# Two blocks of an attention and mixture-of-experts network on one core: block 1's recurrence taken two chunks at a time, and heads' products issued in pairs

## The chip, the cores and the metric

The kernel runs on one core of a Trainium2 chip. The metric is the device time of one launch in microseconds (us); the comparison is between medians of several launches. TensorE is called PE, VectorE DVE, ScalarE ACT, GpSimd POOL and SyncE SP, as the profile calls them.

## The reference, cut to what matters

The input is one sequence of 512 tokens of width 1024. Block 1 projects it (`h @ w_in`), runs a gated recurrence (HGRN2) and a differential attention beside each other, gates and mixes both, and then runs a mixture of experts. Block 2 does the same with an RWKV-7 recurrence and a sparse attention (DSA), followed by a cross attention and a second mixture of experts. The change touches three of these parts:

```
def hgrn2_chunked(q, k, v, log_f):          # 4 heads of 128, 8 chunks of 64 tokens
    def step(state, inp):
        scores = where(causal, q_rel @ k_rel^T, 0)          # 64 x 64 per head
        o = scores @ v + (q * exp(b)) @ state
        new_state = exp(b_end) * state + k_end^T @ v         # 128 x 128 per head
        return new_state, o
o_hg = rms_norm(o, hg_out_norm) * silu(og)

def block(i):                                # differential attention, 4 heads, 128 queries
    a = softmax(q1 @ k1^T) - lam * softmax(q2 @ k2^T)       # q, k of 64 features
    return a @ v
o_da = rms_norm(o_da, da_out_norm) * (1 - lam_init)

s = q_lat @ c_sel^T                          # DSA, 8 heads of 64 features, masked softmax
a = sigmoid(a0 + xa @ a2); w = w0 + tanh(xw) @ w2            # RWKV-7: two products of 64 inner
```

## The kernel before, in words

Everything is float32. A large projection is computed by `mm3` (L209 in the profile): three 128x512 matmuls for each 128 rows of weights, on a high and a low part of each operand. A text that says **dense matmul** means one of these. The weights arrive from HBM in slots and are split by ACT (L194) and DVE (L195). All other matmuls have plain float32 operands, and the trace shows each of them as two passes. Four PSUM banks, d0 to d3, belong to the projections of block 1; the other four, a0 to a3, to the small work.

The order of the instructions on every engine is not written out: a scheduler (the Tile framework with a simulated timeline) places them when the kernel is built. It takes an instruction as soon as its inputs and its buffers are ready in its own simulation, so that PE fills the waits of the small work with dense matmuls. `keep_in_program_order` ties an instruction to the one issued before it in the program. `bank("a")` takes the next bank of a rotation, which `banks(...)` sets.

Block 1 (`dense1`) projects q and k, v, the recurrence's inputs, four gates (`gate(i)`, L691) and the output gate `og`, 1056 dense matmuls in all. `ev_og` takes the four banks of `og` through a Tanh (L700), multiplies on DVE (L701) and then on POOL by the recurrence's normed output (L702), and only with that are d0 to d3 free for `ev_da` and `ev_hg`, the two output projections of 96 dense matmuls each.

The attention (L546 to L571) goes over four heads and four blocks of 128 queries. For each it multiplies the two halves of 64 features (m = 0 and 1), into bank a0 for the one and a1 for the other (L550), adds the mask (L551), runs the softmax, transposes the result through bank a2 (L564) and multiplies by v (L568). Sums of squares for the norm follow for all heads at the end (`tok_sums`, L308).

The recurrence has bank a3 for itself. It goes over four steps of 128 tokens (m), each with scores (L643) and transposes (L648) for two chunks of 64, and then takes the chunks p = 0 and 1 one after the other: state products with 64 inner rows (L658), the state update on DVE (L661), and for every head a product of scores and v (L666) and one of state and q (L667). Its norm (`out_norm`, L677 to L683) follows at the end with its own sums and their spread over the features (`tok_spread`, L319).

Block 2 (`dense2`) runs two small products of 64 inner rows in the RWKV part (L1322, L1326). DSA goes over four pairs of heads (p) and four blocks of queries: scores of the two heads in three banks by turns (L1679), mask (L1682), softmax (L1684 to L1689), transposes through another bank (L1692) and the product with v into d3 (L1698).

## Time and profile before

| | us |
|---|---|
| three launches | 2192.49, 2194.12, 2199.74 |
| median | 2194.12 |
| the profiled execution, device time | 2193.93 |
| its span in the trace | 2192.2 |
| PE busy | 2116.7 (97% of the span) |
| mean granted PE clock | 0.981 of full speed |
| block 1 from its dense matmul #384 to #1056 | 110.9 to 369.2 |
| block 1's output projections | 369.2 to 416.6 |

The profiled execution lies 0.2 us under the median, and 1.7 us of it lie outside the span. The profile gives for each engine its busy time, for each group of instructions its mean time, and for any stretch the granted clock of PE.

### The profile page before, as it was taken

What the parts mean: (1) busy time and instruction counts of PE and PEld (TensorE: products, weight loads), DVE (VectorE), ACT (ScalarE), POOL (GpSimd) and SP (SyncE); (2) the same over time, 40 slices, a digit from 0 to 9 for tenths busy, and PEclk for the clock granted to TensorE, in tenths of its full rate; (3) what the DMA queues carried; (4) which work ended last, traced back from release to release, by engine and by line L of the source; (5) the groups of instructions that cost most, each with busy time, mean ns of one, the idle gap of its engine ahead of it and who ended that gap; (6) DMA issues with size and microseconds to landing.
All of it is one profiled execution on the core that took longest, in us unless ns stands there. A gap on an engine that the chain in (4) does not pass through costs nothing. (4 is left out here: it accounts for less than half of the span.)

```text
span 2192.2 us, 29816 instructions
## 1 busy us (share of the span) xinstructions
PE 2116.7 (97%) x11946; PEld 1363.0 (62%) x11946; DVE 983.7 (45%) x2002; ACT 679.4 (31%) x1317; POOL 161.6 (7%) x138
## 2 busy tenths in 40 slices
PE   8999999999999999998989999999898999999996
PEld 6766778787544444445766775677778454444443
DVE  4674323563333332325388484445455232333334
ACT  5463333253111111114534333433443111111112
POOL 0420001200000000000252100001110000000000
PEclk9999899999999999998999999999999999999998
DMA  4211131377999999993222112112633899999994
GB/s 178 87 66 48 46 109 67 143 287 269 415 419 417 420 420 419 420 377 106 68 76 77 40 63 77 39 65 77 250 110 141 345 409 420 420 419 420 419 419 162
DMA packets 96318, 505.87 MB, mean 231 GB/s; under 512 B 21088, under 2 KB 26208, under 8 KB 44464
## 3 DMA queue, kind: packets, MB, share of 16 engines
q1 hardware_dynamic: 90992, 490.09, 56.3%
q10 hardware_dynamic: 4688, 11.66, 1.5%
q0 software_dynamic: 496, 2.17, 0.3%
q8 instruction: 96, 1.57, 0.3%
q14 instruction: 46, 0.38, 0.0%
HBM read 494.83 MB, written 8.91 MB: 230 GB/s over the span
## 5 line engine op out<-in xcount | busy, mean ns | idle before, releaser
L209 PE MATMUL ps_d<-wslot,xg 128*64 128x512 f32 x2048 | 446.4, 592 | 0.0
L209 PE MATMUL ps_d<-hT,wh 128*128 128x512 f32 x1056 | 348.0, 414 | 1.9 <-DVE hT L300 1.9
L209 PEld LDWEIGHTS ps_d<-wslot,xg 128*64 128x64 f32 x2048 | 148.3, 137 | 286.5 <-issue 276.5
L195 DVE TENSOR_TENSOR wl<-wslot,wh 128x512 fp32r<-128x512 f32 x236 | 168.6, 719 | 287.4 <-ACT wh L194 232.0
L194 ACT ACTIVATE wh<-wslot 128x512 fp32r<-128x512 f32 x260 | 163.2, 630 | 320.9 <-PE ps_d L209 255.8
L209 PEld LDWEIGHTS ps_d<-hT,wh 128*128 128x128 f32 x1056 | 199.7, 195 | 54.7 <-issue 9.3
L1010 DVE TENSOR_TENSOR s<-ps_d,s 128x512 f32<-128x512 f32 x32 | 22.1, 692 | 423.0 <-PE ps_d L209 423.0
L209 PE MATMUL ps_d<-hT,wl 128*128 128x512 f32 x528 | 210.3, 410 | 0.5 <-DVE wl L195 0.5
L209 PE MATMUL ps_a<-wslot,hidT 128*64 128x512 f32 (+1 forms) x832 | 178.3, 578 | 1.7 <-ACT hidT L1018 1.4
L209 PE MATMUL ps_d<-wh,hT 128*128 128x512 f32 x512 | 164.1, 397 | 3.0 <-DVE hT L300 1.4
L1048 DVE TENSOR_TENSOR acc<-acc,ps_a 128x512 f32<-128x512 f32 (+1 forms) x214 | 131.2, 664 | 54.9 <-PE ps_a L209 54.7
L209 PEld LDWEIGHTS ps_a<-wslot,hidT 128*64 128x64 f32 x832 | 58.7, 137 | 108.9 <-issue 100.4
L209 PE MATMUL ps_a<-yy,S 128*128 128x512 f32 (+1 forms) x428 | 114.6, 400 | 5.6 <-DVE acc L1048 5.6
L209 PEld LDWEIGHTS ps_d<-hT,wl 128*128 128x128 f32 x528 | 102.7, 195 | 25.4 <-issue 1.9
L209 PEld LDWEIGHTS ps_d<-wh,hT 128*128 128x128 f32 x512 | 95.7, 188 | 26.7 <-ACT wh L194 1.7
L985 ACT ACTIVATE xg<-ps_a,gain 128x256 f32<-128x256 f32 x102 | 48.2, 475 | 200.0 <-PE ps_a L209 200.0
L209 PE MATMUL ps_a<-oh,xs 128*128 128x256 f32 x816 | 107.1, 285 | 1.3 <-DVE oh L1137 1.3
L209 PEld LDWEIGHTS ps_a<-oh,xs 128*128 128x128 f32 x816 | 100.9, 191 | 9.6 <-issue 9.6
L1036 ACT ACTIVATE yy<-ps_a,gc 128x512 fp32r<-128x512 f32 (+1 forms) x52 | 34.9, 671 | 223.7 <-PE ps_a L209 192.2
L209 PE MATMUL ps_d<-wl,hT 128*128 128x512 f32 x256 | 101.8, 397 | 1.8 <-DVE wl L195 1.8
L209 PEld LDWEIGHTS ps_a<-yy,S 128*128 128x128 f32 x428 | 74.8, 188 | 31.4 <-DVE acc L1048 13.6
L1009 ACT ACTIVATE s<-ps_d 128x512 f32<-128x512 f32 x32 | 19.1, 598 | 199.3 <-PE ps_d L209 199.3
(584 smaller groups left out, 2838.2 us busy)
## 6 DMA issues: line engine op xcount, KB each, us to landing
wslot<-in_wm_dram SPq DMA_DIRECT2D x380, 1024.0 KB, 11.6
wslot<-in_wd_dram SPq DMA_DIRECT2D x108, 512.0 KB, 3.6
wslot<-in_wd_dram SPq DMA_DIRECT2D x19, 1024.0 KB, 14.7
wslot<-in_wm_dram SPq DMA_DIRECT2D x8, 512.0 KB, 15.0
C<-in_x_dram SPq DMA_DIRECT2D x4, 512.0 KB, 5.2
acc<-in_x_dram ACTq DMA_DIRECT2D x4, 512.0 KB, 4.8
kvd<-kvs ACTq DMA_DIRECT2D x8, 256.0 KB, 4.1
xd<-acc ACTq DMA_DIRECT2D x1, 2048.0 KB, 11.9
```

Of the source, the lines that this page charges most:

```text
L194: self.nc.scalar.activation(hi, src, AF.Copy)
L195: (lo_eng or self.nc.vector).tensor_sub(lo, src, hi.bitcast(F32))
L209: self.pin(self.nc.tensor.matmul(*a, **k))
L985: nc.scalar.activation(xg[:, k, :n], b[:, :n], AF.Copy, scale=gain[:, k:k + 1])
L1009: nc.scalar.activation(s1, hb[0], AF.Silu)
L1010: nc.vector.tensor_mul(s1, hb[1], s1)
L1036: nc.scalar.activation(y[0][:, c], b, AF.Copy, scale=gcol)
L1048: nc.vector.tensor_add(acc[:, t, c], acc[:, t, c], b)
```

## The change

A new helper issues a list of products in reversed order and ties all but the first to program order. It is meant for two products with 64 inner rows each, which use the lower and the upper half of PE's rows. Since only the second of two is tied, the scheduler may still put other work between them.

```
+    def side_by_side(self, xs, stop=True):
+        for j, (o, l, r) in enumerate(xs[::-1]):
+            i = self.nc.tensor.matmul(o, l, r, start=True, stop=stop)
+            if j:
+                self.tc.keep_in_program_order(i)
```

In the attention the two score products go through it, into two banks of a rotation of a0 to a3; the transposes reuse the first of these banks, and each head's squares and sums follow its product with v.

```
-                for m in range(2):
-                    r = slice(m * 64, (m + 1) * 64)
-                    b = self.bank("a%d" % m)
-                    nc.tensor.matmul(b[:, :n], qkT[r, 0, h, qs], qkT[r, 1, h, :n], start=True, stop=False)
+                ps, sb = [], [self.bank("a") for _ in range(2)]
+                self.side_by_side([(sb[m][:, :n], qkT[m * 64:m * 64 + 64, 0, h, qs], qkT[m * 64:m * 64 + 64, 1, h, :n])
+                                   for m in range(2)], stop=False)
...
-                b = self.bank("a2")
+                b = sb[0]
...
+            sq = k4([128, 512])
+            nc.scalar.activation(sq, b, AF.Square)
+            b = self.bank("a", (128, 4, 2))
+            self.tok_sums(b, sq, 0, one2)
+            nc.vector.tensor_copy(rd[:, :, 2 * h:2 * h + 2], b)
```

The recurrence loses its own bank and uses the same rotation. A step takes 128 tokens: the state products of both chunks in pairs, eight state updates, one output bank with a product over 128 inner rows of the masked scores (whose off-diagonal halves were zeroed once by POOL) and the products of both states, one copy and one square of the whole step, and its sums.

```
-        self.banks("a3")
...
+            Ss = [S]
+            bks = [self.bank("a", (128, 4, 128)) for _ in range(2 if m < 3 else 1)]
+            for h in range(4):
+                hc = slice(h * 128, (h + 1) * 128)
+                self.side_by_side([(bk[:, h, :], ke[rs[p], h, :], hv[rs[p], m, hc]) for p, bk in enumerate(bks)])
+            for p, bk in enumerate(bks):
+                S = B.tile([128, 4, 128], F32, name="hgS", bufs=3)
+                for h in range(4):
+                    nc.vector.scalar_tensor_tensor(S[:, h, :], Ss[p][:, h, :], eend[:, h, 2 * m + p:2 * m + p + 1],
+                                                   bk[:, h, :], op0=ALU.mult, op1=ALU.add)
+                Ss.append(S)
+            bo = self.bank("a", (128, 4, 128))
+            for h in range(4):
+                nc.tensor.matmul(bo[:, h, :], hv[:, m, h * 128:(h + 1) * 128], sc[:, h, :], start=(h == 0), stop=False,
+                                 skip_group_check=True)
             for p in range(2):
...
                 for h in range(4):
...
+                    nc.tensor.matmul(bo[:, h, rs[p]], Ss[p][:, h, :], qe[:, h, cs[p]], start=False, stop=(p == 1 and h == 3),
+                                     skip_group_check=True)
+            nc.scalar.activation(oT[:, :, tok], bo, AF.Copy)
+            sq = k2([128, 4, 128])
+            nc.scalar.activation(sq, bo, AF.Square)
```

In block 2 the two products of the RWKV part and DSA's scores go through the helper; DSA's pairs alternate between d0, d1 and d2, a2, the transposes reuse the bank of the scores, and the product with v alternates between d3 and a3.

```
-                    b = self.bank(("d0", "d1", "a2")[(turn + e) % 3])
-                    nc.tensor.matmul(b[:, :n], qT[r, p, qs], KT[r, p, :n], start=True, stop=False)
-                    sb.append(b)
+                sb = [self.bank((("d0", "d1"), ("d2", "a2"))[turn % 2][e]) for e in range(2)]
+                turn += 1
+                self.side_by_side([(sb[e][:, :n], qT[e * 64:e * 64 + 64, p, qs], KT[e * 64:e * 64 + 64, p, :n])
+                                   for e in range(2)], stop=False)
...
-                    b = self.bank(("d2", "a3")[turn % 2])
```

**The order on PE, in the recurrence.** The next rows are PE's order of before around one chunk of the recurrence (bank a3); `ps_d...` with hT and wh or wl are dense matmuls of a gate.

```order
L209 MATMUL ps_d2_2321<-hT0_91,wh_2409 128x512
L209 MATMUL ps_d2_2321<-hT1_92,wh_2409 128x512
L209 MATMUL ps_d2_2321<-hT0_91,wl_2410 128x512
L666 MATMUL ps_a3_1898<-k2_1879,F_1534 128x64
L667 MATMUL ps_a3_1898<-E_1389,hgS_1855 128x64
L666 MATMUL ps_a3_1898<-k2_1879,F_1534 128x64
L667 MATMUL ps_a3_1898<-E_1389,hgS_1855 128x64
L666 MATMUL ps_a3_1898<-k2_1879,F_1534 128x64
L667 MATMUL ps_a3_1898<-E_1389,hgS_1855 128x64
L666 MATMUL ps_a3_1898<-k2_1879,F_1534 128x64
L667 MATMUL ps_a3_1898<-E_1389,hgS_1855 128x64
L209 MATMUL ps_d3_2322<-hT0_91,wh_2409 128x512
```

The next rows are PE's order of the change in the recurrence's first and second step (L684 is state and q, L656 the scores, L663 the transposes, L691 the sums, L680 scores and v, L215 the pairs). The dense matmuls at their head are the last of the output gate.

```order
L209 MATMUL ps_d3_2591<-hT0_91,wh_2712 128x512
L209 MATMUL ps_d3_2591<-hT1_92,wh_2712 128x512
L209 MATMUL ps_d3_2591<-hT0_91,wl_2713 128x512
L684 MATMUL ps_a0_1788<-E_1380,hgS_1778 128x64 x4
L656 MATMUL ps_a2_1810<-acc_61 64x64 x8
L663 MATMUL ps_a3_1821<-cst_62,D_1235 128x128 x4
L691 MATMUL ps_a1_1804<-one2_680,k2_1802 128x2 x4
L680 MATMUL ps_a2_1848<-k3_1747,F_1525 128x128 x4
L684 MATMUL ps_a2_1848<-E_1380,hgS_1783 128x64 x4
L215 MATMUL ps_a1_1829<-F_1525,k2_1826 128x128
L215 MATMUL ps_a0_1828<-F_1525,k2_1826 128x128
```

Before, the eight products of a chunk stood between dense matmuls. Now the whole recurrence from here on stands in one row, with no dense matmul among it: dense #1056 is the last one ahead of it.

**The order at the recurrence's end, on PE and ACT.** The next rows are PE's order of the change where the last step ends and the projection of the attention (`ps_d0` from C) begins.

```order
L691 MATMUL ps_a1_1924<-one2_680,k2_1922 128x2 x4
L215 MATMUL ps_a0_1948<-F_1525,k2_1946 128x128 x4
L680 MATMUL ps_a1_1958<-k3_1747,F_1525 128x128 x4
L684 MATMUL ps_a1_1958<-E_1380,hgS_1903 128x64 x4
L684 MATMUL ps_a1_1958<-E_1380,hgS_1953 128x64 x4
L691 MATMUL ps_a2_1974<-one2_680,k2_1972 128x2 x4
L209 MATMUL ps_d0_2754<-C_1196,wh_2760 128x512 x2
L209 MATMUL ps_d0_2754<-C_1196,wl_2761 128x512
```

On ACT the change has this row there (L686 the step's copy, L688 its square, L713 the Tanh of the output gate, L549 the norm's square root, L194 splits).

```order
L686 ACTIVATE G_1742<-ps_a1_1958 128x4x128
L688 ACTIVATE k2_1972<-ps_a1_1958 128x512
L713 ACT_TABLE_LOAD
L713 ACTIVATE k2_2728<-ps_d0_2588 128x512
L713 ACTIVATE k2_2734<-ps_d1_2589 128x512
L713 ACTIVATE k2_2740<-ps_d2_2590 128x512
L549 ACT_TABLE_LOAD
L549 ACTIVATE onr_1745<-onr_1745,eps_65 128x32
L194 ACTIVATE D_2586<-k2_2728 128x512
L194 ACTIVATE D_2586<-k2_2734 128x512
L713 ACT_TABLE_LOAD
L713 ACTIVATE k2_2746<-ps_d3_2591 128x512
```

Before, ACT had this row at the output gate (L700 its Tanh, L679 the norm's square root).

```order
L679 ACT_TABLE_LOAD
L679 ACTIVATE onr_1976<-ps_a3_1977,eps_65 128x32
L194 ACTIVATE wh_2734<-wslot_2716 128x512
L194 ACTIVATE wh_2782<-wslot_2780 128x512
L194 ACTIVATE wh_2798<-wslot_2780 128x512
L700 ACT_TABLE_LOAD
L700 ACTIVATE k2_2750<-ps_d0_2610 128x512
L700 ACTIVATE k2_2756<-ps_d1_2611 128x512
L700 ACTIVATE k2_2762<-ps_d2_2612 128x512
L194 ACTIVATE wh_2816<-wslot_2814 128x512
L194 ACTIVATE D_2608<-k2_2750 128x512
L700 ACTIVATE k2_2768<-ps_d3_2613 128x512
```

The Tanh of the output gate, which frees d0 to d3, now stands behind the last square of the recurrence, and the norm's square root between its third and its fourth Tanh.

**The order on PE, at DSA's end.** The next rows are PE's order of the change in DSA's last two blocks of queries (L215 a pair of scores, L1691 the mask, L1700 transposes, L1705 the product with v; the first row is the last dense matmul of the projection beside it).

```order
L209 MATMUL ps_a1_11178<-r_10011,wl_11198 128x512
L1700 MATMUL ps_a2_10672<-cst_62,k3_10690 128x128 x2
L1700 MATMUL ps_d0_10701<-cst_62,k3_10709 128x128 x3
L1705 MATMUL ps_a3_10644<-GG1_10253,X2_8907 64x128 x4
L215 MATMUL ps_a2_10736<-VU_10008,qT_8933 128x512
L215 MATMUL ps_d2_10735<-VU_10008,qT_8933 128x512
L1691 LDWEIGHTS X4_7459
L1691 MATMUL ps_d2_10735<-X4_7459 128x512
L1691 LDWEIGHTS X4_7459
L1691 MATMUL ps_a2_10736<-X4_7459 128x512
L1705 MATMUL ps_a3_10644<-GG1_10253,X2_8907 64x128
L1700 MATMUL ps_d1_10702<-cst_62,k3_10721 128x128 x3
```

Before, PE's order at the product with v of the last head pair was this one.

```order
L1698 MATMUL ps_d3_10690<-GG1_10275,X2_8929 64x128 x5
L1692 MATMUL ps_a3_10813<-cst_62,k3_10809 128x128 x4
L1698 MATMUL ps_d3_10690<-GG1_10275,X2_8929 64x128
L209 MATMUL ps_a0_11193<-r_10033,wh_11197 128x512
L209 MATMUL ps_a0_11193<-k_10034,wh_11197 128x512
L209 MATMUL ps_a0_11193<-r_10033,wl_11198 128x512
L209 MATMUL ps_a0_11193<-r_10033,wh_11197 128x512
L209 MATMUL ps_a0_11193<-k_10034,wh_11197 128x512
```

The last dense matmul of the projection beside DSA now stands ahead of DSA's last pair, and behind it 16 transposes, 18 products with v, the pair and two masks follow before the next projection begins. Before, 48 dense matmuls stood behind the last transposes, 27 of them behind the last product with v. In the whole order of the change 15 of DSA's 16 pairs stand next to each other, 5 of the attention's 16 (one of 128 and four of 256 keys), all 12 of the recurrence, and one of the four in the RWKV part.

## Rows read from the trace of the kernel before

**Rows 1.** The page, busy time and share of PE.

```profile
PE 2116.7 (97%) x11946; PEld 1363.0 (62%) x11946; DVE 983.7 (45%) x2002; ACT 679.4 (31%) x1317; POOL 161.6 (7%) x138
```

**Rows 2.** Stretches: us, busy us (count) of PE, PEld, DVE, ACT, POOL, granted clock, DMA.

```profile
110.90:369.20 258.30, 257.82 (x1193) 191.30 (x1192) 109.49 (x234) 107.38 (x219) 11.22 (x8) 0.95 0.19 64
369.20:416.60 47.40, 46.87 (x205) 36.86 (x203) 31.52 (x45) 15.81 (x27) 12.22 (x8) 1.00 0.26 87
1343.70:1450.00 106.30, 106.30 (x518) 66.96 (x518) 46.41 (x149) 47.87 (x125) 0.00 (x0) 1.00 0.14 45
```

**Rows 3.** Groups by line in 110 to 420 us: busy us, mean ns.

```profile
L667 PE MATMUL ps_a<-E,hgS 128*128 128x64 f32 x64 | 14.3, 307 | 0.0
L666 PE MATMUL ps_a<-k,F 64*128 64x64 f32 x64 | 13.8, 296 | 0.0
...
L658 PE MATMUL ps_a<-F,k 64*128 64x128 f32 x56 | 8.3, 286 | 0.0
L308 PE MATMUL ps_a<-one,k 128*128 128x2 f32 x64 | 8.3, 256 | 0.0
...
L661 DVE SCALAR_TENSOR_TENSOR hgS<-hgS,eend,ps_a 128x128 f32<-128x128 f32 x28 | 7.9, 342 | 6.9 <-PE ps_a L658 6.8
...
L702 POOL TENSOR_TENSOR k<-k,G 128x512 f32<-128x512 f32 x4 | 5.8, 1455 | 216.2 <-PE ps_a L319 209.4 <-DVE G L683 6.8
L643 PE MATMUL ps_a<-acc 128*64 128x64 f32 x64 | 3.5, 231 | 0.0
...
L700 ACT ACTIVATE k<-ps_d 128x512 f32<-128x512 f32 x4 | 2.2, 599 | 2.2 <-DVE E L195 2.2
...
L700 ACT ACT_TABLE_LOAD x1 | 1.3, 1283 | 0.0
```

**Rows 4.** Timeline of PE, one chunk of the recurrence: start, us, engine, line.

```profile
249.09 0.62 PE L209 MATMUL ps_d<-hT,wh 128*128 128x512 f32 x2
249.65 0.43 PE L666 MATMUL ps_a<-k,F 64*128 64x64 f32 x2
...
252.19 1.68 PE L308 MATMUL ps_a<-one,k 128*128 128x2 f32 x8
```

**Rows 5.** Busy time and granted clock of two neighbouring stretches there.

```profile
249.10:252.40 3.30, 3.30 (x19) 2.47 (x17) 0.69 (x1) 1.88 (x2) 0.00 (x0) 1.00 0.29 94
252.50:259.20 6.70, 6.70 (x21) 5.64 (x21) 0.52 (x2) 1.30 (x3) 0.00 (x0) 0.50 0.08 28
```

**Rows 6.** Timeline of PE at the lower clock, dense matmuls in steps.

```profile
202.42 1.05 PE L209 MATMUL ps_d<-hT,wh 128*128 128x512 f32 x2
203.27 0.84 PE L564 MATMUL ps_a<-cst,k 128*128 128x128 f32 x3
```

**Rows 7.** Timeline of PE, sums of squares at the full clock.

```profile
239.34 1.40 PE L308 MATMUL ps_a<-one,k 128*128 128x2 f32 x12
240.67 1.16 PE L658 MATMUL ps_a<-F,k 64*128 64x128 f32 x8
```

**Rows 8.** Timeline of PE, two products on different halves of its rows.

```profile
206.82 0.37 PE L658 MATMUL ps_a<-F,k 64*128 64x128 f32 x1
206.82 0.48 PE L550 MATMUL ps_a<-C 64*128 64x256 f32 x1
...
207.45 0.23 PE L551 MATMUL ps_a<-dgn,idb 128*128 128x128 bf16 x1
```

**Rows 9.** Timeline of all engines, score products and a reduction in DSA.

```profile
1434.38 0.91 PE L1679 MATMUL ps_a<-VU,qT 64*128 64x384 f32 x2
1435.21 0.44 PE L1692 MATMUL ps_d<-cst,k 128*128 128x128 f32 x2
...
1435.74 1.12 PE L1679 MATMUL ps_d<-VU,qT 64*128 64x512 f32 x2
1436.80 0.39 PE L1682 MATMUL ps_d<-X 128*128 128x512 bf16 x1
...
1437.23 0.69 DVE L1684 TENSOR_REDUCE st<-ps_d 128x1 f32<-128x512 f32 x1 [0.29 <-PE ps_d L1682]
```

More of the change, by code (lines that the diff above doesn't have):

```diff
@@ L569, in dense1 @@
             nc.scalar.activation(vh, b.rearrange("p (j n) -> p j n", j=4), AF.Copy)
[L570 removed]
+            sq = k4([128, 512])
[3 more added lines that the diff above has]
+            nc.vector.tensor_copy(rd[:, :, 2 * h:2 * h + 2], b)
         yd = big("C", (128, 2, 4, 512), F32R)
         vv = lambda h: dv[:, :, h * 128:(h + 1) * 128]
[L573 to L574 removed]
+        scales(rd)
         for h in range(4):
[L576 to L582 removed]
+            b = self.tok_spread(rd, 2 * h, 1)
             o = k3([128, 512])
@@ L634, in dense1 @@
         oT = big("G")
-        S = B.tile([128, 4, 128], F32, name="hgS", bufs=2)
+        S = B.tile([128, 4, 128], F32, name="hgS", bufs=3)
         nc.vector.memset(S, 0.0)
+        rh = A.tile([128, 4, 8], F32, name="onr", bufs=2)
+        scs = [k3([128, 4, 128]) for _ in range(2)]
+        for t in scs:
+            nc.gpsimd.memset(t, 0.0)
         for m in range(4):
             tok = slice(m * 128, (m + 1) * 128)
+            cs = [slice(m * 128 + p * 64, m * 128 + p * 64 + 64) for p in range(2)]
+            rs = [slice(p * 64, p * 64 + 64) for p in range(2)]
             b = self.bank("a", (128, 4, 64))
@@ L641, in dense1 @@
                 for p in range(2):
-                    c = slice(m * 128 + p * 64, m * 128 + p * 64 + 64)
-                    nc.tensor.matmul(b[p * 64:(p + 1) * 64, h, :], krel[:, h, c], qrel[:, h, c], start=True, stop=True)
-            sc = k2([128, 4, 64])
-            nc.vector.tensor_mul(sc, b, self.c("inc64")[:, None, :].broadcast_to([128, 4, 64]))
+                    nc.tensor.matmul(b[rs[p], h, :], krel[:, h, cs[p]], qrel[:, h, cs[p]], start=True, stop=True)
+            sc = scs[m % 2]
+            for p in range(2):
+                nc.vector.tensor_mul(sc[rs[p], :, rs[p]], b[rs[p]],
+                                     self.c("inc64")[rs[p], None, :].broadcast_to([64, 4, 64]))
             b = self.bank("a", (128, 4, 128))
@@ L669, in dense1 @@
-        self.d("o_hgT", oT)
-        def out_norm(o, gcol, out):
-            r = A.tile([128, 4, 8], F32, name="onr", bufs=2)
-            b = self.bank("a", (128, 4, 8))
-            for h in range(4):
-                sq = k2([128, 512])
-                nc.scalar.activation(sq, o(h), AF.Square)
-                self.tok_sums(b, sq, 2 * h, one2)
-            nc.scalar.activation(r, b, AF.Sqrt, scale=1.0 / 128, bias=self.eps)
-            nc.vector.reciprocal(r, r)
-            for h in range(4):
-                b = self.tok_spread(r, 2 * h, 1)
-                nc.vector.scalar_tensor_tensor(out(h), o(h), gcol, b, op0=ALU.mult, op1=ALU.mult)
@@ new lines, in dense1 @@
+            nc.scalar.activation(oT[:, :, tok], bo, AF.Copy)
+            sq = k2([128, 4, 128])
+            nc.scalar.activation(sq, bo, AF.Square)
+            b = self.bank("a", (128, 8))
+            for h in range(4):
+                nc.tensor.matmul(b[:, 2 * h:2 * h + 2], sq[:, h, :], one2, start=True, stop=True)
+            nc.vector.tensor_copy(rh[:, m, :], b)
+        self.d("o_hgT", oT)
+        scales(rh)
+        for h in range(4):
+            b = self.tok_spread(rh, 2 * h, 1)
+            nc.vector.scalar_tensor_tensor(oT[:, h, :], oT[:, h, :], gh[:, 0:1], b, op0=ALU.mult, op1=ALU.mult)
@@ L1320, in dense2 @@
             pc = slice(p * 128, (p + 1) * 128)
-            b = self.bank("a")
-            nc.tensor.matmul(b, lora[0:64, pc], xw[0:64], start=True, stop=True)
+            wb = [self.bank("a") for _ in range(2)]
+            self.side_by_side([(wb[e], lora[e * 64:e * 64 + 64, pc], xw[e * 64:e * 64 + 64]) for e in range(2)])
             ld = tmp[:, p, 0]
-            nc.scalar.activation(ld, b, AF.Tanh, scale=0.5, bias=hw0[:, p:p + 1])
-            b = self.bank("a")
-            nc.tensor.matmul(b, lora[64:128, pc], xw[64:128], start=True, stop=True)
+            nc.scalar.activation(ld, wb[0], AF.Tanh, scale=0.5, bias=hw0[:, p:p + 1])
             th = tmp[:, p, 1]
-            nc.scalar.activation(th, b, AF.Tanh, scale=0.5, bias=ha0[:, p:p + 1])
+            nc.scalar.activation(th, wb[1], AF.Tanh, scale=0.5, bias=ha0[:, p:p + 1])
             nc.gpsimd.tensor_scalar(ld, ld, hc, hc, op0=ALU.mult, op1=ALU.add)
@@ L1670, in dense2 @@
         for p in range(4):
-            bo_ = self.bank("d3")
+            bo_ = self.bank(("d3", "a3")[p % 2])
             for i in range(4):
@@ L1693, in dense2 @@
                     nc.scalar.activation(pTs[:, e, i, :n], b[:, :n], AF.Copy)
-                    turn += 1
                 for j in range(i + 1):
```

39 lines of the change are left out of this document (7 added, 32 removed).

## The prediction, written before the changed kernel ran

> **What bounds the kernel now.** I read the page first: PE is busy for 2116.7 of 2192.2 us, 97% [rows 1], and DVE follows with 45%. So time is won where PE does less or does it at a higher clock, and lost where it has to wait. Then the stretches that the change touches [rows 2]. In block 1, from 110.9 to 369.2 us, PE is busy for 257.82 of 258.30 us, but its granted clock is 0.95; in the output projections behind it and in DSA PE is as full, at 1.00, so that there too PE time saved is time saved. The reader is to see that the small work's waits on DVE and ACT cost nothing there: dense matmuls stand in every gap. Last I read how the clock falls. [...] In block 1 I count eight such stretches of 3.4 us (27.2 us at 0.50 make a mean of 0.947, the 0.95 of the row), each behind a burst of L666, L667 or L308, short matmuls that stand together. A dense matmul there takes 427 ns (202.42 to 203.27 us for two, [rows 6]), at the full clock some 230 (the output projections: 205 matmuls, nearly all of them dense, in 46.87 us, [rows 2]).
>
> **What block 1 loses.** L666 and L667 take 2.54 us a chunk when they stand in a burst [rows 4], eight times 20.3 us; their busy times, which overlap, sum to 28.1 us [rows 3]. I take 23, nearer to the burst, since most chunks are one. L658 goes (8.0, little under its busy 8.3), L643 (3.2 of 3.5) and L648 (16 passes, 1.8, as L308 takes 0.11 us a pass at full clock: 1.33 us for 12, [rows 7]), and the recurrence's half of L308, 32 passes, 3.6. Together 39.6 us. With the bursts gone I also take the eight half-clock stretches away: 3.4 us hold eight dense matmuls of 427 instead of 231 ns, 1.56 us each, 12.5 in all. Of the attention's pairs only five stand next to each other in the new order. A single score product takes 0.83 us for 384 keys (1434.38 to 1435.21) and 1.06 for 512 [rows 9], so 0.22 for 128 keys: about 0.61 for 256 and 0.39 for 128. That two products on different halves of the rows run beside each other is seen once: L658 and L550 both begin at 206.82 us, and all four passes are over at about 207.45 [rows 8], when one L550 of 256 keys alone would take 0.61 us. So a pair costs one product: five pairs give 0.39 + 4 x 0.61 = 2.8 us. Block 1 loses 54.9 us.
>
> **What block 1 gains.** The order shows that from the last dense matmul of the output gate, #1056, to the end of the recurrence no dense matmul is left to fill in. The reason stands in ACT's row: the Tanh that empties banks d0 to d3 comes behind the recurrence's last square. So this stretch is the sum of PE's work and its waits. By the passes (L308's 0.111 us; L643 0.05, 3.2 us for 64), a step of 128 tokens has 8 passes each of scores and v, state one, state two, transposes and sums, 0.9 each or 4.4 with the transposes a little cheaper; 16 passes of scores, 0.8; four pairs, 1.1 (L658's 8.3 us are 0.15 a pass, eight passes one after the other). 6.3 us in all. Behind the pairs PE waits for the first state's four updates: 0.35 us until DVE starts (0.43 after the start of the last matmul that it waits for, [rows 9]), four times 342 ns [rows 3] and, an estimate by the first, 0.1 back to PE, 1.8 us. A step then is 8.1 us at full clock and, with PE's part at 1.92 times, 13.9 at half clock. Which? The stretch is one long burst of the kind behind which the clock fell, so I let it fall in the middle of the second step: 11.0 there, 13.9 in the third, and 12.1 in the fourth, where the wait lies behind two other groups. With the first step's products at the full clock (2.9), the last state's (1.7) and the tail (ACT's copy, square and Tanh at 0.6 each like L700, a table load of 1.28 [rows 3], DVE's product of 0.69 like its reduction in [rows 9], hand-overs 0.65: 4.4) this makes 46.0 us. Ahead of #1056 stand the first scores and transposes, 1.6. The dense matmuls behind begin at half clock, 2.0 (eight to ten of them). Then bank d3 comes late: its Tanh needs a buffer that POOL frees. From the spread's first bank, DVE's product of 0.7, POOL's 1.45 [rows 3], a split of 1.3 (a pass of ACT and one of DVE), the table load and Tanh of 1.9 and DVE's 0.7, with 1.75 of first matmuls and hand-overs, are 7.8 us, of which PE fills 4.5 with the rest of the spread and five dense matmuls; 3.3 remain. Block 1 gains 52.9 us, and so is 2.0 faster in sum.
>
> [...] The shortest passes decide this sum: L308 streams two columns and takes 0.111 us a pass [rows 7]. [...]
>
> **Block 2.** In DSA 15 of 16 pairs stand together. One group of four lengths costs 0.39 + 0.61 + 0.83 + 1.06 = 2.9 us, four times 11.5; without the one pair of 256 keys, 10.9 us less. In the RWKV part one pair of four gives 1.05, the price of one product of 512 columns. A product with 64 inner rows between dense matmuls also costs something at its entry: two dense matmuls ahead of L666 take 0.56 instead of 0.46 us (249.09 to 249.65, [rows 4]). Twenty-one entries fewer, 2.0 us. Against this, DSA's last part has no filler any more: 48 dense matmuls stood behind its last transposes and none do now. Its chain from the last dense matmul on is five transposes and four products with v (2.0 us), the pair and masks (1.6), a softmax of 512 keys and the rest of the other head's (the reduction is 0.69 [rows 9], the exponential about the same, then it is read, inverted and scaled: 3.3 with hand-overs, an estimate by these passes), transposes and copy 1.5, eight products 1.7, and copy and split of the next operand 2.6: 12.7 us. PE has 9.0 of work in it, 3.7 are wait, and with some of the work at half clock I take 4.5 (0 if the next projection's operands come early, 8 if all of it runs at half clock). Sum: -10.9 - 1.05 - 2.0 + 4.5 = -9.5 us.
>
> **The sum.** -2.0 - 9.5 = -11.5 us against the profiled 2193.93, which is 0.2 under the median: about 2182. Both MoE parts and the transfers keep their order, so the shift carries through to the end.
>
> **The rivals.** (a) The clock stays at 1.00 in the recurrence's stretch: 8.1 + 8.1 + 6.6 + 2.9 + 0.9 + 4.4 = 31.0 us instead of 46.0, and 2.0 less behind it, 17 us: **2165**. For it speaks that the stretch has no idle long enough to be seen; against it, that the clock fell behind bursts a tenth as long. (b) The clock is low from the first step (+3) and the attention, with its own L308 and short matmuls, keeps four of the eight half-clock stretches (+6): **2191**, within what can be told. (c) In the stretch nothing overlaps: beside the 1.8 us, the mask (0.9), the transposes' copy (1.0), the output's copy and square (1.6) and the second state's updates wait one after the other, and a step at half clock takes 12.1 + 1.8 + 0.9 + 1.0 + 1.6 + 1.8 = 19 us instead of 14. That is 57 + 9 = 66 us, 20 more: **2202**, slower. It decides from 17.8 us a step on (2200.5). The order speaks against it: sums and the next scores stand between. (d) The pairs don't run beside each other: 10.9 + 1.05 + 2.8 + 2.0 and 4.8 in the recurrence come back, 21.5: **2203**. Against it stands the one overlap at 206.82, for it that this is only one.
>
> **How the numbers follow.** A difference under 0.3%, 6.6 us, can't be told from no change here. My own case has 0.50 and its own range is 2176 to 2189 (the stretch between 42 and 49 us, DSA's tail between 0 and 8); 0.44 of it lies under 2187.5. (a) has 0.15, (b) 0.17, (c) 0.11, (d) 0.07. The range from 2163 to 2196 leaves (c) and (d) out. Faster: 0.44 + 0.15 = 0.59; same 0.06 + 0.17 = 0.23; slower 0.18.
>
> **What the changed profile would show.** Block 1 from dense #384 to #1248 takes about as long as before (305 us). Between #1056 and #1057 there are some 45 us without L209, with a clock of about 0.55; 31 us at 1.00 would be (a), 60 and more (c). Before it, the clock up to #1056 is 1.00; with 0.50 stretches still there, (b). A DSA pair of 512 keys takes 1.06 us, not 2.1 (d). Behind DSA's last dense matmul PE is idle for about 4 us. I would be wrong most of all in the clock of the recurrence, which alone is worth 17 us, and in the half-clock stretches that I let go, 12.5 us.

## The result, and the profile after

The changed kernel takes 2170.49 us (median of 4 launches, 2167.89 to 2170.81) against 2195.49 us before (4 launches): ratio 0.9885, 95% interval 0.9868 to 0.9902, 25 us or 1.15% faster. The forecast was 2182, 11.5 us faster, with a range from 2163 to 2196; the time lies in it, three fifths of the way from the forecast to its low end, and the gain is a little over twice the one forecast. The profiled execution took 2170.49 us, its span is 2168.5 us.

The page of the changed kernel answers to [rows 1]: PE is 37 us less busy and its share of the span is a little lower.

```profile
PE 2079.4 (96%) x11910; PEld 1348.1 (62%) x11914; DVE 986.8 (46%) x2014; ACT 676.4 (31%) x1313; POOL 162.5 (7%) x140
```

To see where the time went I take the starts of the same dense matmuls (L209, 128x512) in both traces, counted from the kernel's first one. The forecast column is the prediction's sum by place: the 54.9 us that block 1 loses and 0.5 for the attention's entries, less 1.6 ahead of #1056; the 46.0 us of the recurrence's stretch; 2.0 and 3.3 behind it; and block 2's terms.

| stretch of PE (starts of dense matmuls) | before, us | after, us | difference | forecast |
|---|---|---|---|---|
| start to #384 | 110.5 | 109.2 | -1.3 | 0 |
| #384 to #1056: attention, and before the recurrence too | 258.3 | 204.8 | -53.5 | -53.8 |
| #1056 to #1057: the bare recurrence | 0.8 | 25.6 | +24.8 | +46.0 |
| #1057 to #1248: output projections | 46.6 | 56.0 | +9.4 | +5.3 |
| #1248 to #4022: first MoE, block 2's RWKV part | 910.0 | 917.4 | +7.4 | -1.2 |
| #4022 to #4313: DSA | 141.2 | 129.2 | -12.0 | -8 |
| #4313 to the end | 724.7 | 726.3 | +1.6 | 0 |

The windows of the changed kernel answer to [rows 2] and [rows 5]. Columns: stretch, length, busy us and count of PE, PEld, DVE, ACT and POOL, granted clock of PE, DMA share and GB/s.

```profile
109.30:314.40 205.10, 205.10 (x952) 153.49 (x951) 104.52 (x216) 95.37 (x201) 13.14 (x10) 1.00 0.22 75
314.40:339.70 25.30, 20.97 (x214) 18.98 (x212) 9.94 (x32) 9.30 (x16) 0.00 (x0) 0.96 0.23 84
339.70:344.50 4.80, 4.80 (x11) 3.76 (x12) 1.53 (x4) 1.77 (x3) 0.00 (x0) 0.50 0.00 0
344.50:354.50 10.00, 5.74 (x33) 4.62 (x31) 5.97 (x8) 3.66 (x5) 4.19 (x3) 0.99 0.00 1
354.50:360.00 5.50, 5.41 (x17) 4.29 (x18) 3.23 (x6) 2.42 (x4) 1.67 (x1) 0.69 0.28 93
```

The attention's stretch runs at 1.00 throughout: the eight half-clock stretches are gone. The recurrence is bare, as the order told, but its clock is 0.96, not 0.55: in this profile it falls only at the stretch's end, at 337.9 us (e1, below, has it earlier). What is lost behind it is the low clock (339.7 to 344.5) and a wait of 4.3 us. One step of the recurrence, in the rows of PE and DVE:

```profile
318.34 1.00 PE L684 MATMUL ps_a<-E,hgS 128*128 128x64 f32 x8
319.27 1.16 PE L215 MATMUL ps_a<-F,k 64*128 64x128 f32 x16
320.48 2.15 DVE L675 SCALAR_TENSOR_TENSOR hgS<-hgS,eend,ps_a 128x128 f32<-128x128 f32 x8 [2.77 <-PE ps_a L215]
320.88 1.21 PE L684 MATMUL ps_a<-E,hgS 128*128 128x64 f32 x8 [0.45 <-DVE hgS L675]
```

PE waits 0.45 us and not 1.8: the first head's product starts at 320.88 us, 0.05 us behind the end of the first of the four updates (320.83) and ahead of the fourth's (321.35). And the wait for bank d3:

```profile
348.73 4.19 POOL L715 TENSOR_TENSOR k<-k,G 128x512 f32<-128x512 f32 x3 [44.91 <-DVE G L697]
...
350.05 0.63 ACT L194 ACTIVATE D<-k 128x512 fp32r<-128x512 f32 x1 [8.55 <-POOL k L715]
...
351.28 0.63 ACT L194 ACTIVATE D<-k 128x512 fp32r<-128x512 f32 x1 [0.60 <-POOL k L715]
351.93 1.28 ACT L713 ACT_TABLE_LOAD   x1
353.22 0.60 ACT L713 ACTIVATE k<-ps_d 128x512 f32<-128x512 f32 x1
...
354.59 0.94 PE L209 MATMUL ps_d<-C,wh 128*128 128x512 f32 x2 [4.35 <-DVE k L714]
```

The chain is the one forecast; the second split (351.28), which stands ahead of the table load on ACT and waits for POOL, was left out of it.

In DSA a pair of 512 keys and the end stand in PE's timeline, which answers to [rows 9].

```profile
1433.39 0.69 PE L215 MATMUL ps_a<-VU,qT 64*128 64x512 f32 x1
1433.40 0.69 PE L215 MATMUL ps_d<-VU,qT 64*128 64x512 f32 x1
1433.92 0.59 PE L215 MATMUL ps_a<-VU,qT 64*128 64x512 f32 x1
1433.93 0.59 PE L215 MATMUL ps_d<-VU,qT 64*128 64x512 f32 x1
1434.68 0.38 PE L1691 MATMUL ps_a<-X 128*128 128x512 bf16 x1 [0.16 <-issue]
...
1442.24 0.96 PE L209 MATMUL ps_d<-GG,wh 128*128 128x512 f32 x3 [1.20 <-ACT GG L194]
```

Both products of the pair start 0.01 us apart and are over after 1.1 us, the time of one (1.12 us in [rows 9]); in the records of the 15 pairs the starts are 6 to 8 ns apart. From here to the next projection PE waits for ACT and DVE four times (0.58, 0.62, 0.24 and 1.20 us), and once ahead of the pair (0.41), 3.05 us in all.

### The profile page after: what moved, and what is told of

Same layout as the page of the kernel before. It is cut to its first block, busy times and chain, and to the rows that moved or that the text cites. A ratio compares the mean times of both kernels' runs of the same rounds, so it can differ in the third digit from the quotient of the medians.

```text
span 2168.5 us, 29754 instructions
## 1 busy us (share of the span) xinstructions
PE 2079.4 (96%) x11910; PEld 1348.1 (62%) x11914; DVE 986.8 (46%) x2014; ACT 676.4 (31%) x1313; POOL 162.5 (7%) x140
## 5 line engine op out<-in xcount | busy, mean ns | idle before, releaser
L209 PE MATMUL ps_d<-wslot,xg 128*64 128x512 f32 x2048 | 446.4, 592 | 0.0
L209 PE MATMUL ps_d<-hT,wh 128*128 128x512 f32 x1056 | 344.2, 410 | 2.8 <-DVE hT L308 2.8
L209 PEld LDWEIGHTS ps_d<-wslot,xg 128*64 128x64 f32 x2048 | 148.3, 137 | 286.5 <-issue 277.1
L194 ACT ACTIVATE wh<-wslot 128x512 fp32r<-128x512 f32 x260 | 163.2, 631 | 310.0 <-PE ps_d L209 239.8
L209 PEld LDWEIGHTS ps_d<-hT,wh 128*128 128x128 f32 x1056 | 197.5, 193 | 54.4 <-issue 9.3
L209 PE MATMUL ps_d<-hT,wl 128*128 128x512 f32 x528 | 205.7, 402 | 0.0
L209 PE MATMUL ps_a<-wslot,hidT 128*64 128x512 f32 (+1 forms) x832 | 178.3, 578 | 1.7 <-ACT hidT L1031 1.4
L209 PE MATMUL ps_d<-wh,hT 128*128 128x512 f32 x512 | 163.8, 397 | 3.1 <-ACT wh L194 1.4
L1061 DVE TENSOR_TENSOR acc<-acc,ps_a 128x512 f32<-128x512 f32 (+1 forms) x214 | 131.2, 664 | 54.9 <-PE ps_a L209 54.7
L209 PEld LDWEIGHTS ps_a<-wslot,hidT 128*64 128x64 f32 x832 | 58.7, 137 | 108.9 <-issue 100.4
L209 PE MATMUL ps_a<-yy,S 128*128 128x512 f32 (+1 forms) x428 | 114.6, 400 | 5.6 <-DVE acc L1061 5.6
L209 PEld LDWEIGHTS ps_d<-hT,wl 128*128 128x128 f32 x528 | 101.3, 192 | 24.0 <-issue 1.5
L209 PEld LDWEIGHTS ps_d<-wh,hT 128*128 128x128 f32 x512 | 95.6, 188 | 26.9 <-ACT wh L194 1.8
L209 PE MATMUL ps_a<-oh,xs 128*128 128x256 f32 x816 | 107.1, 285 | 1.4 <-DVE oh L1150 1.4
L209 PEld LDWEIGHTS ps_a<-oh,xs 128*128 128x128 f32 x816 | 100.9, 191 | 9.6 <-issue 9.6
L209 PE MATMUL ps_d<-wl,hT 128*128 128x512 f32 x256 | 101.3, 396 | 1.8 <-DVE wl L195 1.8
L209 PEld LDWEIGHTS ps_a<-yy,S 128*128 128x128 f32 x428 | 74.8, 188 | 31.4 <-DVE acc L1061 13.5
## 6 DMA issues: line engine op xcount, KB each, us to landing
wslot<-in_wd_dram SPq DMA_DIRECT2D x19, 1024.0 KB, 15.2
```

What stands on the lines that cost most here:

```text
L194: self.nc.scalar.activation(hi, src, AF.Copy)
L209: self.pin(self.nc.tensor.matmul(*a, **k))
L1061: nc.vector.tensor_add(acc[:, t, c], acc[:, t, c], b)
```

## The experiments

Each ran against the kernel before, on one chip for both. The stages are those of the table above; block 1 and bare are lengths, in us.

| run | median, us | before, us | ratio, 95% | block 1 (#384 to #1248) | bare (#1056 to #1057) | #1248 to #4022 | DSA |
|---|---|---|---|---|---|---|---|
| before | | | | 305.7 | 0.8 | 910.0 | 141.2 |
| the change | 2170.49 | 2195.49 | 0.9885 (0.9868 to 0.9902) | 286.4 | 25.6 | 917.4 | 129.2 |
| e1, again | 2169.34 | 2192.23 | 0.9892 (0.9878 to 0.9907) | 288.6 | 28.4 | 910.9 | 129.2 |
| e2, block 2 only | 2181.79 | 2192.23 | 0.9950 (0.9935 to 0.9964) | 304.3 | 0.8 | 909.6 | 129.2 |
| e3, recurrence only | 2173.98 | 2192.23 | 0.9916 (0.9902 to 0.9930) | 278.3 | 0.8 | 913.7 | 141.2 |
| e4, gate's own buffer | 2157.85 | 2192.23 | 0.9840 (0.9824 to 0.9856) | 275.5 | 0.2 | 912.2 | 129.2 |
| e5, attention undone | 2159.67 | 2193.67 | 0.9849 (0.9831 to 0.9868) | 278.0 | 0.8 | 912.7 | 129.2 |
| e6, attention's pairs | 2157.31 | 2193.67 | 0.9829 (0.9809 to 0.9848) | 273.4 | 9.8 | 918.8 | 129.2 |
| e7, pairs apart | 2180.49 | 2193.67 | 0.9950 (0.9936 to 0.9964) | 288.7 | 28.3 | 911.1 | 142.5 |
| e8, chunks alternate | 2195.33 | 2193.67 | 1.0007 (0.9993 to 1.0020) | 310.6 | 45.3 | 917.0 | 129.2 |
| e9, alternate, 128 rows | 2176.98 | 2195.11 | 0.9911 (0.9892 to 0.9930) | 295.1 | 30.6 | 916.6 | 129.2 |
| e10, pairs and buffer | 2139.87 | 2195.11 | 0.9755 (0.9737 to 0.9773) | 263.7 | 0.2 | 910.9 | 129.2 |
| e11, before, sorted | 2180.73 | 2195.32 | 0.9938 (0.9922 to 0.9954) | 289.9 | 0.8 | 911.1 | 141.2 |
| e12, DSA's tail | 2142.92 | 2195.32 | 0.9768 (0.9749 to 0.9787) | 262.1 | 0.2 | 916.3 | 128.7 |

### The parts by themselves: e1, e2, e3, e5

**e1, the changed kernel again.** No edit.

> The changed kernel itself once more. It was 25 us faster, twice the 11.5 forecast. Theory A: 19 us came from block 1 (no half-clock stretches, a recurrence that kept the full clock), 12 from DSA's pairs, and stages that the change doesn't touch gave some 6 us back by longer half-clock stretches that differ from execution to execution. Then the time is 2168 to 2172 again, and this profile shows block 1 (dense #384 to #1248) at 286 us, DSA (from its first score product to the next projection) at 112, and the losses in the untouched stages at other places or of other size. Rival: those losses belong to the new order; then they stand in this profile where they stood before, within 0.3 us each.

The time came again, and so did DSA. The 7.4 us lost between #1248 and #4022 did not: 910.9 us here, as before. So they don't belong to the order. They go with low clock in stages whose instructions are the same: between #1248 and #4022 the clock is 0.50 for 47.8 us in the changed kernel's first profile and for 30.7 us in that of before. In the first MoE's routing, for instance, the changed kernel's first profile had one half-clock stretch that the kernel before had not; the windows of the changed kernel and then of before over the same matmuls:

```profile
440.00:480.90 40.90, 39.59 (x282) 37.51 (x282) 25.83 (x80) 23.45 (x42) 5.27 (x2) 0.96 0.57 212
```

```profile
461.00:500.00 39.00, 37.65 (x280) 35.53 (x278) 25.54 (x80) 22.84 (x41) 5.28 (x2) 1.00 0.58 214
```

Over the fourteen profiles the stage from #1248 to #4022 is between 909.6 and 918.8 us, with and without block 2's change.

Block 1 takes 288.6 us and not 286.4, because the clock of the bare stretch is not the same in the two profiles of this kernel. Here it falls at 333.2 us, in the fourth step and 18.5 us behind #1056, and the stretch takes 28.4 us:

```profile
314.70:333.20 18.50, 16.86 (x180) 15.18 (x179) 8.04 (x26) 5.68 (x10) 0.00 (x0) 1.00 0.13 41
333.20:346.90 13.70, 11.77 (x45) 10.49 (x45) 3.43 (x9) 5.55 (x8) 0.00 (x0) 0.50 0.25 100
```

In e7, whose matmuls in block 1 stand in the same order, it falls at 333.3 us, also for 13.7 us. So of three profiles of this order one has the fall 23.8 us behind #1056, at the stretch's end, and two have it 5 us earlier.

**e2, block 2 only.** The edits of the attention and the recurrence are taken back.

> Only the changes in block 2 (DSA and the two small products of the RWKV part), block 1 as before. Theory A: DSA's pairs give 12 us by themselves, so about 2183; block 1 stays at 305.7 us with its eight half-clock stretches. Rival: the pairs don't run beside each other and DSA is faster only because its banks come free sooner; then a pair of 512 keys takes 2.1 us in the trace and the time is above 2188.

10.4 us faster. DSA is 12.0 us shorter in the trace; the two small products of the RWKV part give nothing that can be seen (909.6 against 910.0).

**e3, recurrence only.** The attention and block 2 as before; the recurrence as changed, on all four banks:

```
-        self.banks("a3")
+        self.banks("a0", "a1", "a2", "a3")     # ahead of the changed recurrence
```

> Only the recurrence's change (two chunks a step, rotation of four banks, early sums), attention and block 2 as before. Theory A: block 1's gain is nearly all from here, 16 of the 19 us: 2178, no half-clock stretch up to the last dense matmul of the output gate, and again a bare stretch of 25 us at the full clock behind it. Rival: the attention's rotation over four banks and its early sums made the order that has no half-clock stretches; then they are back here and the time is 2188 or more.

18.3 us faster, more than expected, and block 1 is 8 us shorter than with the whole change. The bare stretch isn't there: #1057 follows #1056 after 0.8 us. With the attention's old order its last product with v starts at 245.8 us, not at 286.6, and the recurrence's steps (264 to 329 us in the trace) stand among dense matmuls. The clock is 1.00 all the same, in the windows up to #1056 and behind it:

```profile
112.20:341.60 229.40, 228.92 (x1171) 173.39 (x1170) 114.91 (x245) 105.79 (x215) 12.40 (x10) 1.00 0.21 73
341.60:390.50 48.90, 46.42 (x194) 35.56 (x193) 31.05 (x41) 16.04 (x28) 12.23 (x8) 1.00 0.25 82
```

**e5, attention undone.** The changed kernel with the attention's edits taken back.

> The changed kernel with the attention as before (its own three banks, single score products, sums at the end), new recurrence and new block 2. The parts measured so far: recurrence alone 18.3 us faster, block 2 alone 10.4, the whole change only 22.9, so the attention's part should cost 5.8. Theory A: it does, because with four banks by turns the attention ends later (dense #966 instead of #699) and shuts the recurrence out to where no dense matmul is left; then this is 2163 to 2165 and the recurrence stands among dense matmuls. Rival: the parts' gains don't add (half-clock stretches fall elsewhere when the order moves); then 2168 or more.

34 us faster than before, some 10 faster than the whole change and 3 below what theory A had. The attention's part as a whole (rotation, early sums and pairs) is a loss here, and the table shows its place: without it the bare 25 us don't exist.

### The pairs: e7 and e6

**e7, pairs apart.**

```
-                self.side_by_side([...], stop=False)
-                for e, b in enumerate(sb):
-                    nc.tensor.matmul(b[:, :n], idb, ..., start=False, stop=True)
+                for e in (1, 0):                  # score, mask, score, mask, in this order
+                    x = nc.tensor.matmul(sb[e][:, :n], qT[...], KT[...], start=True, stop=False)
+                    if e == 0: self.tc.keep_in_program_order(x)
+                    x = nc.tensor.matmul(sb[e][:, :n], idb, ..., start=False, stop=True)
+                    if e == 1: self.tc.keep_in_program_order(x)
+                for e, b in enumerate(sb):
```

> The changed kernel with the mask of the first head placed between the two score products of every DSA pair, nothing else. Theory A: DSA's 12 us come from products that run beside each other; apart, each costs its own time again: 15 pairs, 10.9 us, and 15 entries of 0.1: about 2181. Rival: DSA gained by its banks (transposes into the scores' bank, two pairs of banks by turns) and not by the overlap: 2172 or less.

As theory A has it: DSA takes 142.5 us, 13.3 more. Its last 2.7 us are at half clock, with PE idle for 1.2 of them; that makes under 1 us of these. In PE's timeline each product has its 1.05 us to itself:

```profile
1412.49 1.12 PE L1689 MATMUL ps_a<-VU,qT 64*128 64x512 f32 x2
1413.54 0.39 PE L1693 MATMUL ps_a<-X 128*128 128x512 bf16 x1
1413.86 1.12 PE L1689 MATMUL ps_d<-VU,qT 64*128 64x512 f32 x2
1414.91 0.39 PE L1693 MATMUL ps_d<-X 128*128 128x512 bf16 x1
```

**e6, the attention's pairs on two banks.** On the kernel of e5:

```
-                for m in range(2):
-                    r = slice(m * 64, (m + 1) * 64)
-                    b = self.bank("a%d" % m)
-                    nc.tensor.matmul(b[:, :n], qkT[r, 0, h, qs], qkT[r, 1, h, :n], start=True, stop=False)
+                sb = [self.bank("a%d" % m) for m in range(2)]
+                self.side_by_side([...], stop=False)
+                for m, b in enumerate(sb):
```

> As the run with the attention undone, but its score products issued as pairs into banks a0 and a1, one for each half as before; by the order all 16 pairs stand together (5 in the changed kernel). Theory A: each pair costs one product, so 4 x 2.9 = 11.5 us of PE go, 1 to 2 come back as the recurrence ends later: about 2153. Rival: the attention's chain through its three banks sets its end, the pairs free PE only for dense matmuls that are then missing behind the recurrence: 2160 or more.

Between the two: 2157, where e5 has 2160. All 16 pairs stand together, but block 1 gains only 4.6 of 11 us, since the recurrence's end is bare again, for 9.8 us, PE waits behind it, and the clock falls once there (339.4 us, for 6.8). The windows of block 1 show both:

```profile
317.80:327.60 9.80, 8.46 (x79) 7.67 (x77) 4.90 (x16) 4.45 (x9) 0.00 (x0) 1.00 0.58 215
327.60:382.80 55.20, 49.86 (x207) 39.22 (x208) 32.33 (x45) 17.99 (x28) 11.72 (x8) 0.94 0.19 63
```

### The bare stretch: e4, e10, e12

**e4, a buffer of its own for the output gate.**

```
+        og = B.tile([128, 4, 512], F32, name="aT", bufs=2)
         def ev_og(j, b):
-            s = k2([128, 512])
+            s = og[:, j, :]
```

> The changed kernel, with a buffer of its own for the output gate's Tanh (that of the attention's last transposed probabilities but one), so that banks d0 to d3 come free before the recurrence and the attention's projection can stand among its steps. Theory A: the bare stretch (4.3 us of waits), the wait of 4.35 us for bank d3 and the half-clock stretches behind both (about 4) go, and 7 us come back where the norm's end has no filler any more: 5 us faster than the changed kernel, 2165. Rival: with dense matmuls among the short ones the clock falls again as it did before the change: 2170 or more.

11.5 us faster than the changed kernel in the same comparison, twice the 5 expected. The rival has no support: the clock is 1.00 while short and dense matmuls stand mixed. In its windows the wait is gone up to 350 us and 2.5 us are left at the end:

```profile
314.00:350.30 36.30, 36.30 (x261) 30.94 (x260) 18.06 (x43) 10.21 (x18) 0.00 (x0) 1.00 0.18 59
350.30:384.70 34.40, 31.87 (x162) 26.63 (x160) 23.08 (x34) 13.21 (x21) 12.30 (x8) 0.95 0.30 107
```

**e10, both.** The kernel of e6 with e4's buffer.

> As the run with all the attention's pairs, with the output gate's own buffer in addition, so that the attention's projection can stand among the recurrence's last steps. In that run the recurrence's end stood bare for 9.8 us (dense #1056 to #1057), with two half-clock stretches behind it. Theory A: both go, 12 us: 2145 to 2149. Rival: the bare part only moves behind the attention's projection, as the norm's end and the splits for the last projection have no filler then: 2153 or more.

2139.87 us, 2.45% under the kernel before, 5 us below theory A's range and the fastest here. Block 1 takes 263.7 us, PE is busy for 263.1 of them:

```profile
109.30:317.60 208.30, 208.30 (x1085) 162.07 (x1084) 108.27 (x231) 101.18 (x210) 14.00 (x10) 0.99 0.22 74
317.60:349.30 31.70, 31.70 (x189) 27.18 (x188) 16.25 (x34) 10.67 (x18) 2.73 (x2) 1.00 0.35 126
349.30:373.00 23.70, 23.11 (x97) 18.01 (x97) 18.25 (x25) 9.38 (x15) 9.50 (x7) 1.00 0.22 77
```

**e12, DSA's tail.** The kernel of e10, with the last 24 dense matmuls beside DSA queued behind DSA's last pair:

```
+                with tc.issue_after(lastp.ins) if i + x == 2 else ExitStack():
-                self.dense256(4, ya, ev_a, wk, 3, ("a0", "a1"))
+                    self.dense256(4, ya, ev_a, wk, 3, ("a0", "a1"))
```

> As the fastest run so far (all pairs, the output gate's own buffer, 2140 us), with the last 24 dense matmuls beside DSA queued behind DSA's last pair of scores. Theory A: the 3.7 us that PE waits in DSA's last part are filled, 3 us faster: 2136 to 2138. Rival: the dense matmuls are missing where they stood before, ahead of the last pair, and the wait moves there: 2139 to 2142.

The rival holds: DSA is 0.5 us shorter, and the time, 1 us above the rival's range, is not lower. PE still waits 3.25 us in DSA, and 2.0 of them stand now ahead of the last pair (1400.5 to 1403.7 us), where the filler was taken away.

### The clock: e8, e9, e11

**e8, chunks alternate.** The changed kernel, in whose recurrence scores and v are multiplied again over 64 rows, by turns with state and q; a second bank and ACT's copies and squares in halves come with it.

```
+            for p in range(2):
+                bo = self.bank("a", (128, 4, 64))
+                for h in range(4):
+                    nc.tensor.matmul(bo[:, h, :], hv[rs[p], m, h * 128:(h + 1) * 128], sc[rs[p], h, rs[p]], start=True, stop=False)
+                    nc.tensor.matmul(bo[:, h, :], Ss[p][:, h, :], qe[:, h, cs[p]], start=False, stop=True)
```

> The changed kernel, but in the recurrence scores and v are again multiplied chunk by chunk over 64 inner rows, each head's product followed by that of state and q, as before the change; the step's pairs, sums and rotation stay, and the stretch stays bare of dense matmuls. By 2.54 us a chunk instead of 1.4 it costs 9 us at the full clock. Theory A2 (the clock fell behind chunks of before because products of 64 and 128 inner rows alternate there): half-clock stretches come up inside the bare stretch, 9 us more and 8 to 10 for the clock: 2186 or more. Rival (alternation has nothing to do with it; it is the share of waits or chance): 2179 and the clock stays at 1.00 up to the recurrence's end as in the changed kernel.

The whole gain of the change is gone. PE's timeline shows a product every 0.36 us, and the windows the half clock for the rest of the recurrence:

```profile
316.30 0.43 PE L684 MATMUL ps_a<-E,hgS 128*128 128x64 f32 x2
316.66 0.43 PE L682 MATMUL ps_a<-k,F 64*128 64x64 f32 x2
317.02 0.43 PE L684 MATMUL ps_a<-E,hgS 128*128 128x64 f32 x2
```

```profile
315.50:320.80 5.30, 5.30 (x48) 4.60 (x46) 1.70 (x4) 1.89 (x4) 0.00 (x0) 1.00 0.00 0
320.80:360.70 39.90, 39.90 (x189) 34.33 (x189) 8.66 (x28) 6.86 (x15) 0.00 (x0) 0.50 0.14 53
```

**e9, the same over 128 rows.**

```
-  hv[rs[p], m, h * 128:(h + 1) * 128], sc[rs[p], h, rs[p]]
+  hv[:, m, h * 128:(h + 1) * 128], sc[:, h, rs[p]]
```

> As the run in which chunks alternate (2195 us, at half clock for 44 us from the recurrence's second step on), with the same number, order and width (64 columns) of products, but scores and v are multiplied over all 128 inner rows, half of them zeros, so that all of these products have 128 inner rows. Theory A2 (the clock falls where products of 64 and 128 inner rows alternate): the clock stays at 1.00 in the bare stretch up to its last waits and the time is 2174 to 2180. Rival (the clock falls because the products are short and many, whatever their inner rows): half-clock stretches of 30 us and more again, 2190 or more.

The time is where A2 put it, but not for its whole reason. As many products of the same width now come every 0.22 us, and the clock still falls, later and for 20 us:

```profile
315.42 0.39 PE L684 MATMUL ps_a<-E,hgS 128*128 128x64 f32 x2
315.64 0.39 PE L682 MATMUL ps_a<-k,F 128*128 128x64 f32 x2
```

```profile
314.80:326.20 11.40, 11.34 (x124) 10.56 (x122) 4.87 (x15) 3.80 (x9) 0.00 (x0) 1.00 0.01 1
326.20:333.00 6.80, 6.80 (x41) 6.46 (x40) 1.36 (x6) 0.93 (x3) 0.00 (x0) 0.50 0.00 0
333.00:336.40 3.40, 3.27 (x38) 3.05 (x38) 1.81 (x7) 0.99 (x3) 0.00 (x0) 1.00 0.16 30
336.40:350.10 13.70, 13.30 (x51) 11.92 (x51) 2.41 (x6) 3.62 (x7) 0.00 (x0) 0.50 0.38 147
```

One of its six launches took 2167.91 us at a mean clock of 0.983, the others 2176 to 2179 at 0.975 to 0.979. PE's order is that of e8. So in a bare stretch the clock also fell where scores and v run over 128 rows, as in e1 and e7 too; where they run over 64, by turns with state and q, it fell sooner and for longer (5.3 us behind #1056 and for 44 us in e8, 11.4 and 20 here, 18.5 and 14 in e1).

**e11, the kernel before with its chunk sorted.**

```
                 for h in range(4):
                     vh = hv[r, m, h * 128:(h + 1) * 128]
-                    nc.tensor.matmul(bo[:, h, :], vh, sc[r, h, :], start=True, stop=False)
-                    nc.tensor.matmul(bo[:, h, :], So[:, h, :], qe[:, h, c], start=False, stop=True)
+                    nc.tensor.matmul(bo[:, h, :], vh, sc[r, h, :], start=(h == 0), stop=False, skip_group_check=True)
+                for h in range(4):
+                    nc.tensor.matmul(bo[:, h, :], So[:, h, :], qe[:, h, c], start=False, stop=(h == 3), skip_group_check=True)
```

> The kernel before with one edit: in a chunk of its recurrence the four products of scores and v (64 inner rows) come first and the four of state and q (128) behind them, instead of by turns. Theory A2 (alternation of 64 and 128 inner rows costs time at every turn and brings the clock down): a chunk takes 1.9 instead of 2.54 us, 5 us in all, and most of the eight half-clock stretches go, another 8: 2180 to 2184. Rival (the half-clock stretches come from short products as such): only the 5 us, 2187 to 2190, and the eight stretches stay.

14.6 us by the order of eight products; all other matmuls of PE stand in block 1 as before. Four of 64 rows now take 1.03 us and the others 0.24 each, and of the eight half-clock stretches two are left up to #1056, 3.4 us each. One stands behind this chunk and eight passes of L308, the other behind 24 passes of L308 with no chunk near:

```profile
243.82 1.10 PE L666 MATMUL ps_a<-k,F 64*128 64x64 f32 x8
244.85 0.88 PE L668 MATMUL ps_a<-E,hgS 128*128 128x64 f32 x6
245.57 1.01 PE L308 MATMUL ps_a<-one,k 128*128 128x2 f32 x8
...
336.09 2.73 PE L308 MATMUL ps_a<-one,k 128*128 128x2 f32 x24
```

```profile
246.80:250.20 3.40, 3.40 (x10) 2.62 (x10) 0.35 (x1) 0.47 (x2) 0.00 (x0) 0.50 0.12 43
250.20:339.00 88.80, 88.80 (x481) 72.63 (x480) 26.82 (x50) 30.46 (x52) 0.00 (x0) 1.00 0.28 95
339.00:342.40 3.40, 3.40 (x9) 2.64 (x8) 0.69 (x1) 1.91 (x2) 0.00 (x0) 0.51 0.02 5
```

## Why the prediction was right, and where its sum was off

**What block 1 loses** came out as forecast up to #1056, -53.5 against -53.8 us, with no half-clock stretch left. Part of that is luck. The first step's products, 2.9 us, stand ahead of #1056 in the trace, where the sum had them behind it, so that 56.4 us went:

```profile
310.36 1.16 PE L215 MATMUL ps_a<-F,k 64*128 64x128 f32 x16
...
313.26 0.48 PE L209 MATMUL ps_d<-hT,wl 128*128 128x512 f32 x1
```

And the 2.54 us of [rows 4] hold seven of a chunk's eight products. Eight take 2.9, or 23 us for eight chunks, which is what the sum took in place of 20.3.

The reason given for the half-clock stretches, short matmuls that stand together, tells only a part of what the runs show. In the trace of before the clock falls to 0.50 seven times there (six times for 3.4 us, once for 6.8, [rows 5]), five times behind a chunk, where products of 64 and 128 rows come by turns ([rows 4]), and twice without a chunk: at 242.2 us behind twelve passes of the two-column sums of L308 and eight of L658, and at 354.8 us behind twenty-four of L308 (351.80 to 354.40 us). e11 keeps all the short products and only sorts the chunks, and two falls are left, both with L308 ahead of them.

**The bare stretch** is the term that was mis-sized: 46.0 us forecast from #1056 to #1057, 25.6 measured (28.4 in e1, 28.3 in e7). Its place and its cause (banks d0 to d3 held by the output gate) were right, as e4 shows. Three sizes in it failed. The clock was let fall in the second step; it fell in the fourth or behind it, so rival (a), with 0.15, is nearest, and its 31.0 us are 15 less. What (a) took for itself, that no idle can be seen, did not decide it: in e8 the clock fell at 320.8 us with PE busy for all of the 5.3 us ahead. The 2.9 us of the first step were not there. And the wait for the state was 0.45 us instead of 1.8, in two steps, 2.7 in all. Together these are the 20 us. e8 and e9 suggest why the rows of before misled: most of those bursts were alternating ones, and the change's are not. No row showed the factor 1.92 for the half clock; e9's products give 1.9 (0.43 and 0.22 us), e8's 1.7 (0.62 and 0.36).

**Behind it** the wait for d3 was 4.35 us instead of 3.3, by a second split ahead of the table load, and the low clock came twice, from 337.9 and from 355.0 us, not once: 9.4 instead of 5.3.

**Block 2** gave 12.0 us instead of 8 in DSA. The tail's wait was 3.05 us, near the 3.7 that the chain gave, where the sum took 4.5. PE's work fell by 15.2 us (busy for 141.2 us before, for 126.0 of 129.1 in e1), where the sum had 12.4: 15 pairs at 0.73 and 15 entries at 0.1. The price of a pair was right within what e7 can tell (13.3 us, 0.89 for each of 15, against 0.83). The other 2 us are not explained: with the pairs apart, e7's DSA still has PE busy for 139.2 us, 2.0 less than before. The RWKV part's 1.05 can't be seen.

**The other rivals.** (b) is refuted by the clock of 1.00 up to #1056, (c) by the step's 6.8 us (318.34 to 325.16), (d) by the pair's 1.1 us and by e7. The limit in (c) is 18.4 us a step by its own terms, not 17.8.

**The sum.** -23.7 us between the two profiles is -19.3 in block 1, -12.0 in DSA, -1.3 ahead and 9.0 back in stages that the change doesn't touch; e1 shows that most of these 9 belong to the execution. Block 1 and DSA together gave 31.3 us where the forecast had 10.4. That the profiled time came nearer to the forecast than these parts is chance.

**What was not forecast** is that one of the parts is a loss. The order was read right (the attention ends at #966 and not at #699, the recurrence is bare behind it), but the price was set against the gain of the recurrence as one thing. e3 and e5 separate them: the attention's part costs about 10 us, and these runs don't divide this among rotation, early sums and pairs. Most of it seems to come with the output gate's hold on d0 to d3: e4, with the changed attention and a buffer for the gate, is as fast as e5. The version with the attention's old banks, pairs on fixed banks and that buffer (e10) is 30 us faster than the change.

What stays open is why the clock falls when it does: at 333 us in e1 and e7 and at 337.9 us in the change's first profile, with the same matmuls, and in e9 in five launches of six, as times and mean clocks suggest; only one of them was profiled.

## What to carry to other kernels

Small matmuls that use half of PE's rows were cheap here in pairs (1.12 us for two of 512 columns, as for one; apart, DSA took 13.3 us more, e7) and dear by turns with full ones (0.36 us a product of 64 columns in e8, 0.22 in e9; sorting them took 14.6 us off in e11): put two halves side by side, and sort the rest by their rows. When a part gets new buffers or banks, look in the order at who now stands without filler behind it; one buffer for a late reader (here the output gate) was worth 11.5 us in e4, half of what the whole change gained there. A gain of 1%, 25 us, stands beside a stretch (#1248 to #4022) that took between 909.6 and 918.8 us in the fourteen profiles, so compare stage by stage.
